# First feed-forward: a fourth pair of blocks by seven products, five low parts a group summed by DMA from DRAM

## The chip, the cores and the metric

The kernel runs on one core of a Trainium2 chip. The metric is the device time of one execution in microseconds (us), the median of several. Products run on TensorE (PE; PEld is its loading of weights), sums and splits on VectorE (DVE), casts and scalings on ScalarE (ACT). GpSimd (POOL) issues the DMAs that sum while they write, and SyncE (SP) issues the loads.

## What is computed

One layer of a streaming encoder on 256 tokens of width 2048, in float32:

```python
def swiglu_ffn(h, w_in, w_out):
    gate, up = jnp.split(h @ w_in, 2, axis=-1)
    return (jax.nn.silu(gate) * up) @ w_out

x = x + 0.5 * swiglu_ffn(rms_norm(x, ffn1_norm), ffn1_w_in, ffn1_w_out)   # F = 5632
...                                  # convolution and gating mixers, then cross-attention
x = x + 0.5 * swiglu_ffn(rms_norm(x, ffn2_norm), ffn2_w_in, ffn2_w_out)
return rms_norm(x, final_norm)
```

The change is in `h @ w_in` of the first feed-forward, a product of 256 x 2048 by 2048 x 11264.

## The kernel before

**Split numbers.** A float32 weight tile `raw` (128 x 1024) is split into a high part, which ScalarE casts (L339), and a low part, which VectorE gets as raw - high (L340); both go into a buffer of two planes, `hl`. A product is three matmuls: high x by high w, high x by low w, low x by high w (`three`, `by_two`). x is split once, in `x_hl`.

**Groups.** The 11264 columns are taken in 11 groups of 512 gate and 512 up columns. A group runs over 16 k-tiles of 128 rows, which are eight pairs. Group 0 is plain. In groups 1 to 10 each pair has a letter in `PATTERNS`. A "C" pair (`eight`) takes eight products of 128 tokens by 512 columns, 24 matmuls. An "S" pair (`seven`) takes seven products of sums of blocks, 21 matmuls: VectorE forms sums of weight blocks first (L385, L386, L391, L398) and then splits those too, in three and a half splits. The matching sums of x blocks (`forms`) are made once during group 0, by `sides`.

**Summed low parts.** For the k-tiles in `SUMMED`, which lie in C pairs, VectorE does nothing: ScalarE writes -raw into the low plane (L355) and the cast into the high plane (L356), and a DMA issued by GpSimd adds raw to the low plane, from raw's own buffer (L357). There is one such buffer, `hl_s`; the next k-tile of the list is begun when the matmuls of the one before have been written out.

**Buffers.** Raw tiles come into four buffers of `wraw` and five pieces of `spare`, nine in turn. Splits go to three buffers of `whl` and two of `ring`, five in turn. All eight banks of PSUM hold accumulators, named by the products: "5", "6", "7" and "1" are complete after the last S pair, "2", "3", "4" and "8" after the last pair. VectorE drains the latter four (L449, four instructions a group) and `give` makes the group's output `h`. x itself, `xT` (2 MB), stays in SBUF from group 0 to the output product, which adds to it.

**Order.** The program is written in this order, and a scheduler then fixes the order of each engine's queue when the kernel is built; each queue runs in that order. A waiting instruction holds up what stands behind it on its engine.

Of the kernel before, what the change touches and what calls it, by code (L numbers as in the profile page):

```python
# [17 lines left out]
P = 128  # L18
D = 2048
T = 256  # L20
# [15 lines left out]

PATTERNS = ("SCSCSCCC", "SCSCSCCC")

SUMMED = (2, 7, 13)

# [26 lines left out]
def layer(ctx: ExitStack, tc: tile.TileContext, a: dict):  # L67
# [231 lines left out]
    class FeedForward:  # L299
# [5 lines left out]

        def __init__(self, stack, tags, x_hl, gain, w_in, pattern):
            self.x_hl, self.gain, self.w_in, self.pattern = x_hl, gain, w_in, pattern
            self.tags = tags
            self.spairs = [p for p, c in enumerate(pattern) if c == "S"]
# [20 lines left out]
            self.hA = self.hB = self.hC = None  # L330
            self.hl = self.own.tile([P, 2, 1024], F32R, name="hl_s")
            self.first = self.hl.rearrange("p a (f two n) -> p (a f) two n", f=2, two=2)

        def parts(self, raw, n=1024, last=False):

            i = self.at % 5
            self.at += 1
            hl = whl.tile([P, 2, 1024], F32R, name="hl") if last or i < 3 else self.ring[i - 3]
            nc.scalar.copy(out=hl[:, 0, :n], in_=raw[:, :n])  # L339
            newest[0] = nc.vector.tensor_tensor(  # L340
                out=hl[:, 1, :n], in0=raw[:, :n], in1=hl[:, 0, :n].bitcast(F32), op=ALU.subtract
            )
            return hl
# [7 lines left out]

        def summed(self, j, k):

            raw = self.raw(j, k)
            nc.scalar.activation(out=self.hl[:, 1], in_=raw, func=AF.Copy, scale=-1.0)  # L355
            nc.scalar.copy(out=self.hl[:, 0], in_=raw)  # L356
            nc.gpsimd.dma_start(out=self.hl[:, 1], in_=raw, accum_op=ALU.add)  # L357

# [43 lines left out]
        def eight(self, j, p, b, first, last, plain):  # L402
            for k in (2 * p, 2 * p + 1):
                at = (j, k) in self.sums_at and self.sums_at.index((j, k))
                w = self.parts(self.raw(j, k), last=plain) if at is False else self.hl
# [15 lines left out]
        def group(self, j, r, after=()):  # L421
# [10 lines left out]
            for p, c in enumerate(self.pattern):  # L432
# [8 lines left out]
                else:  # L441
                    late = p > self.spairs[-1] and len(after) > 0
                    self.eight(j, p, b, p == self.pattern.index("C"), p == n - 1, late)
                    if p > self.spairs[-1] + 1:
                        for _ in range(2):
# [5 lines left out]

        def run(self, before, after, root):
            acc = token_accs()
            self.sums_at = [(j, k) for j in range(1, NG) for k in SUMMED if j < NG - 1 or k < SUMMED[-1]]
            for k in range(KD):
# [64 lines left out]
    with ExitStack() as stack:  # L520
        ff = FeedForward(stack, ("S1", "S0", "S2"), x_hl, "ffn1_norm", a["ffn1_w_in"], PATTERNS[0])

# [19 lines left out]

        turns = ff.run(x_arrives, x_more, x_root)

# [419 lines left out]
    with ExitStack() as stack:  # L964
        ff = FeedForward(stack, ("S0", "S1", "S2"), x_hl, "ffn2_norm", a["ffn2_w_in"], PATTERNS[1])
        x2 = ff.x2
# [162 lines left out]
```

## Time and profile before

| | us |
|---|---|
| median of 3 runs (2112.79 to 2116.53) | 2114.3 |
| the profiled execution | 2113.83 |
| its span | 2111.8 |
| TensorE busy in the span | 2084.6 |
| VectorE busy | 1576.2 |
| ScalarE busy | 1156.1 |
| groups 1 to 10 of the first feed-forward | about 55 to 478 |
| groups 1 to 10 of the second feed-forward | about 1434 to 1853 |

Times in the profile count from the start of the span. A row of a timeline has the start, the length, the engine, the line, the operation, what it writes and reads, and in brackets how long the engine was idle before it and which instruction ended that. A row of waits has the engine and line that waited, what it waited for, and us in total, times, and the longest.

### The profile page before, as it was taken

The page shows a single profiled execution, that of the slowest core. Times are in us where ns is not written, and L with a number is a line of the kernel's source. Part 1 is how long each engine was busy: PE and PEld are TensorE (multiplying, and loading weights), DVE is VectorE, ACT ScalarE, POOL GpSimd, SP SyncE. Part 2 cuts the span into 40 slices and gives each one's busy share as a digit, 9 for nine tenths or more (in the row PEclk, how much of TensorE's full clock was granted, in tenths as well). Part 3 has the DMA queues.
Part 4 walks back from the last instruction along what each step waited for, and adds up shares of the span by engine and source line. Part 5 has one row for each costly group of instructions (what it writes and reads, how often), then busy time and mean ns, then how long its engine had stood idle before and what let it go on. Part 6 is the DMA issues. An engine that isn't in the chain of part 4 may idle for free.

```text
span 2111.8 us, 26657 instructions
## 1 busy us (share of the span) xinstructions
PE 2084.6 (99%) x9764; PEld 1737.2 (82%) x9764; DVE 1576.2 (75%) x2215; ACT 1156.1 (55%) x1450; POOL 66.4 (3%) x81
## 2 busy tenths in 40 slices
PE   8999999999999999999999999999999999999998
PEld 6888877888888888888888888888888888888886
DVE  7887888876655589989877665777878888787754
ACT  7656565655544455444764454556665666454443
POOL 0000000000000000000000000000000000000000
PEclk9999999999999999999999999999999999999999
DMA  9788777855666676656565543686788778656664
GB/s 352 219 239 231 238 239 216 262 171 168 218 191 189 201 238 204 187 177 186 174 201 187 184 156 111 206 281 190 232 253 249 217 230 263 180 160 201 195 192 149
DMA packets 121955, 440.24 MB, mean 208 GB/s; under 512 B 13664, under 2 KB 13792, under 8 KB 121696
## 3 DMA queue, kind: packets, MB, share of 16 engines
q1 hardware_dynamic: 113184, 407.35, 59.9%
q0 software_dynamic: 8352, 30.41, 7.8%
q8 instruction: 76, 1.25, 0.2%
q10 hardware_dynamic: 288, 0.79, 0.1%
q14 instruction: 55, 0.45, 0.1%
HBM read 405.99 MB, written 2.10 MB: 193 GB/s over the span
## 4 chain that ended last, share of the span: by engine, by line
PE 70%; issue 25%; DMA 2%; DVE 2%; POOL 1%; ACT 1%; POOLq 0%; SPq 0%; DVEq 0%; ACTq 0%
PE acc L172 12%; PE acc L173 12%; PE acc L171 12%; PE acc L125 8%; PE acc L126 4%; PE acc L288 4%; PE acc L289 4%; PE acc L291 4%; PE aux L263 1%; PE acc L275 1%; PE acc L277 1%; PE acc L276 1%; DMA raw<-in_ffn_w_in 1%; POOL hl_s L357 1%; PE acc L1049 1%
## 5 line engine op out<-in xcount | busy, mean ns | idle before, releaser
L113 DVE TENSOR_TENSOR hl<-raw,hl 128x1024 fp32r<-128x1024 f32 (+1 forms) x402 | 489.0, 1217 | 280.9 <-ACT hl L112 279.8
L112 ACT CAST hl<-raw 128x1024 fp32r<-128x1024 f32 (+1 forms) x402 | 419.6, 1045 | 482.6 <-PE acc L173 300.1
L339 ACT CAST hl<-spare 128x1024 fp32r<-128x1024 f32 (+1 forms) x148 | 143.7, 996 | 117.0 <-DVE spare L386 55.0
L340 DVE TENSOR_TENSOR hl<-spare,hl 128x1024 fp32r<-128x1024 f32 (+1 forms) x148 | 169.7, 1158 | 32.8 <-ACT hl L339 32.2
L288 PE MATMUL acc<-hl,x_hl 128*128 128x512 f32 x440 | 152.7, 392 | 8.3 <-ACT hl L339 8.3
L289 PE MATMUL acc<-hl,x_hl 128*128 128x512 f32 x440 | 159.0, 392 | 0.1
L339 ACT CAST ring<-spare 128x1024 fp32r<-128x1024 f32 (+1 forms) x106 | 103.3, 983 | 97.7 <-DVE spare L386 49.8
L340 DVE TENSOR_TENSOR hl<-raw,hl 128x1024 fp32r<-128x1024 f32 (+1 forms) x106 | 119.6, 1133 | 47.7 <-ACT hl L339 47.0
L339 ACT CAST hl<-raw 128x1024 fp32r<-128x1024 f32 (+1 forms) x106 | 101.9, 975 | 65.4 <-DVE raw L398 27.6
L291 PE MATMUL acc<-hl,x_hl 128*128 128x512 f32 x440 | 136.7, 391 | 0.0
L340 DVE TENSOR_TENSOR ring<-spare,ring 128x1024 fp32r<-128x1024 f32 (+1 forms) x106 | 120.4, 1142 | 21.3 <-ACT ring L339 20.8
L288 PEld LDWEIGHTS acc<-hl,x_hl 128*128 128x128 f32 x440 | 83.0, 189 | 25.8 <-ACT hl L339 8.7
L172 PE MATMUL acc<-hl,x_hl 128*128 128x512 f32 x256 | 100.5, 392 | 0.5 <-DVE hl L113 0.5
L172 PE MATMUL acc<-hl,m_hl 128*128 128x512 f32 x256 | 100.3, 392 | 0.0
L173 PE MATMUL acc<-hl,m_hl 128*128 128x512 f32 x256 | 100.2, 391 | 0.0
L173 PE MATMUL acc<-hl,x_hl 128*128 128x512 f32 x256 | 99.8, 390 | 0.0
L289 PEld LDWEIGHTS acc<-hl,x_hl 128*128 128x128 f32 x440 | 82.9, 189 | 17.9 <-DVE hl L340 0.8
L291 PEld LDWEIGHTS acc<-hl,x_hl 128*128 128x128 f32 x440 | 83.2, 189 | 17.5
L289 PE MATMUL acc<-ring,x_hl 128*128 128x512 f32 x256 | 92.6, 389 | 0.5 <-DVE ring L340 0.5
L171 PE MATMUL acc<-hl,m_hl 128*128 128x512 f32 x256 | 91.2, 392 | 0.0
L125 PE MATMUL acc<-x_hl,hl 128*128 128x512 f32 x256 | 91.0, 398 | 0.0
L125 PE MATMUL acc<-y_hl,hl 128*128 128x512 f32 x256 | 90.5, 399 | 0.0
(326 smaller groups left out, 5066.5 us busy)
## 6 DMA issues: line engine op xcount, KB each, us to landing
spare<-in_ffn_w_in SPq DMA_DIRECT2D x192, 512.0 KB, 5.2
raw<-in_ffn_w_out SPq DMA_DIRECT2D x176, 512.0 KB, 3.8
raw<-in_ffn_w_in SPq DMA_DIRECT2D x160, 512.0 KB, 4.9
hl_s<-spare POOLq DMA_DIRECT2D x32, 512.0 KB, 4.9
raw<-in_w_mix_vg SPq DMA_DIRECT2D x32, 512.0 KB, 4.7
raw<-in_w_k SPq DMA_DIRECT2D x32, 512.0 KB, 3.9
raw<-in_w_v SPq DMA_DIRECT2D x32, 512.0 KB, 4.3
raw<-in_w_mix_out SPq DMA_DIRECT2D x32, 512.0 KB, 4.6
```

Source lines behind the costliest of these rows:

```text
L112: nc.scalar.copy(out=hl[:, 0, :size], in_=raw[:, :size])
L113: newest[0] = nc.vector.tensor_tensor(out=hl[:, 1, :size], in0=raw[:, :size], in1=hl[:, 0, :size].bitcast(F32), op=ALU.subtract)
L125: nc.tensor.matmul(acc, lhsT=w_hi, rhs=x_hl, start=first, stop=False, skip_group_check=True)
L126: nc.tensor.matmul(acc[:, 0], lhsT=w_lo, rhs=x_hl[:, 0], start=False, stop=last, skip_group_check=True)
L171: nc.tensor.matmul(acc[t], lhsT=x[:, 0, s], rhs=hi[:, k], start=k0 + k == 0, stop=False)
L172: nc.tensor.matmul(acc[t], lhsT=x[:, 0, s], rhs=lo[:, k], start=False, stop=False)
L173: nc.tensor.matmul(acc[t], lhsT=x[:, 1, s], rhs=hi[:, k], start=False, stop=k0 + k == nk - 1)
L288: nc.tensor.matmul(acc[t][g], lhsT=x[:, 0, s], rhs=hi[:, cols[g]], start=(t, g) in first, stop=False)
L289: nc.tensor.matmul(acc[t][g], lhsT=x[:, 0, s], rhs=lo[:, cols[g]], start=False, stop=False)
L291: nc.tensor.matmul(acc[t][g], lhsT=x[:, 1, s], rhs=hi[:, cols[g]], start=False, stop=last)
L339: nc.scalar.copy(out=hl[:, 0, :n], in_=raw[:, :n])
L340: newest[0] = nc.vector.tensor_tensor(out=hl[:, 1, :n], in0=raw[:, :n], in1=hl[:, 0, :n].bitcast(F32), op=ALU.subtract)
```

## The change

Pair 5 of the first feed-forward becomes an S pair, so four of eight are. Five k-tiles a group, 2, 6, 12, 14 and 15, have their low part summed by DMA, where three had (2, 7, 13). The summing DMA reads the weights again from DRAM, in both feed-forwards. After group 0, x's place is given to a sixth split buffer and a second summed buffer (tile `more`), and x is loaded again after the last group. The second feed-forward keeps its pattern, its list and its single buffers. Line numbers after L339 move up by 3 or more: the drains are L452, the summing DMA is L360.

```diff
-PATTERNS = ("SCSCSCCC", "SCSCSCCC")
+PATTERNS = ("SCSCSSCC", "SCSCSCCC")
-SUMMED = (2, 7, 13)
+SUMMED = ((2, 6, 12, 14, 15), (2, 7, 13))
...
-            self.hl = self.own.tile([P, 2, 1024], F32R, name="hl_s")
+            self.hls = [self.own.tile([P, 2, 1024], F32R, name="hl_s")]
...
         def parts(self, raw, n=1024, last=False):
-            i = self.at % 5
+            i = self.at % (3 + len(self.ring))
...
-        def summed(self, j, k):
-            raw = self.raw(j, k)
-            nc.scalar.activation(out=self.hl[:, 1], in_=raw, func=AF.Copy, scale=-1.0)
-            nc.scalar.copy(out=self.hl[:, 0], in_=raw)
-            nc.gpsimd.dma_start(out=self.hl[:, 1], in_=raw, accum_op=ALU.add)
+        def summed(self, at):
+            if at >= len(self.sums_at):
+                return
+            j, k = self.sums_at[at]
+            raw, hl = self.raw(j, k), self.hls[at % len(self.hls)]
+            nc.scalar.activation(out=hl[:, 1], in_=raw, func=AF.Copy, scale=-1.0)
+            nc.scalar.copy(out=hl[:, 0], in_=raw)
+            nc.gpsimd.dma_start(out=hl[:, 1], in_=self.w_in[j, :, k], accum_op=ALU.add)
...
-                if at is not False and at + 1 < len(self.sums_at):
-                    self.summed(*self.sums_at[at + 1])
+                if at is not False:
+                    self.summed(at + len(self.hls))
...
-                    self.summed(*self.sums_at[0])
+                    self.summed(0)
+            if more is not None:
+                more()
+                self.summed(1)
...
-            if k in (6, 9, 12):
+            if k in (6, 9, 12, 15):
                 ff.sides(k // 3 - 2)
...
-        turns = ff.run(x_arrives, x_more, x_root)
+        def x_given():
+            more = xt.tile([P, 4, 1024], F32R, name="more", tag="x")
+            ff.ring.append(more[:, :2])
+            ff.hls.append(more[:, 2:])
+
+        turns = ff.run(x_arrives, x_more, x_root, x_given)
+        xT = xt.tile([P, KD, T], F32, name="xT", tag="x")
+        for k in range(0, KD, 8):
+            nc.gpsimd.dma_start(out=xT[:, k:k + 8], in_=a["xT"][:, k:k + 8])
```

How the order of the queues changes is shown at three places. The first is TensorE where group 1 of the first feed-forward ends and group 2 begins (L275 to L277 are S matmuls, L288 to L291 C matmuls; `aux` and `acc` are accumulators; `DMASW` stands for a summing DMA). Before, behind the last C matmuls of group 1, stand the S matmuls of group 2's first pair into banks that are free early (the first four rows are their end), and then, from the fifth row on, the first ones into a drained bank:

```order
L277 MATMUL aux<-hl,ring 128x512
L275 MATMUL acc<-hl,x_hl 128x512
L276 MATMUL acc<-hl,x_hl 128x512
L277 MATMUL acc<-hl,x_hl 128x512
L275 MATMUL acc<-hl,x_hl 128x512 [waits DVE_49,Activation_49]
L276 MATMUL acc<-hl,x_hl 128x512
L277 MATMUL acc<-hl,x_hl 128x512
L288 MATMUL acc<-hl_s,x_hl 128x512 [waits Activation_49]
L289 MATMUL acc<-hl_s,x_hl 128x512 [waits DMASW3_49]
```

Now group 1's last k-tile, summed, stands behind group 2's first twelve matmuls, and the first matmul into a drained bank follows at once:

```order
L275 MATMUL acc<-hl,x_hl 128x512 [waits DVE_49]
L276 MATMUL acc<-hl,x_hl 128x512
L277 MATMUL acc<-hl,x_hl 128x512
L288 MATMUL acc<-hl_s,x_hl 128x512 [waits Activation_49]
L288 MATMUL acc<-hl_s,x_hl 128x512 x3
L289 MATMUL acc<-hl_s,x_hl 128x512 [waits DMASW4_49]
L289 MATMUL acc<-hl_s,x_hl 128x512
L291 MATMUL acc<-hl_s,x_hl 128x512 x2
L289 MATMUL acc<-hl_s,x_hl 128x512 x2
L291 MATMUL acc<-hl_s,x_hl 128x512 x2
L275 MATMUL acc<-hl,x_hl 128x512 [waits DVE_49]
```

The matmuls into banks that are free early moved ahead of the last k-tile, so fewer of them stand between the end of a bank and its next use. The second place is GpSimd, the first five summing DMAs. Before, each reads the buffer of the raw tile and waits for ScalarE and for the load:

```order
L357 DMA hl_s<-spare 128x1024 [waits DMAHW0_49,Activation_49]
L357 DMA hl_s<-raw 128x1024 [waits DMAHW3_49,Activation_49]
L357 DMA hl_s<-spare 128x1024 [waits DMAHW2_49,Activation_49]
L357 DMA hl_s<-raw 128x1024 [waits DMAHW5_49,Activation_49]
L357 DMA hl_s<-spare 128x1024 [waits DMAHW0_49,DVE_49,Activation_49]
```

Now they read DRAM, into two buffers in turn, and wait for ScalarE alone, but for the first into x's place:

```order
L360 DMA hl_s<-in_ffn_w_in 128x1024 [waits Activation_49]
L360 DMA more<-in_ffn_w_in 128x1024 [waits DMAHW3_49,DMAHW2_49,DMAHW4_49,DMAHW0_49,DMAHW7_49,DVE_49,Activation_49]
L360 DMA hl_s<-in_ffn_w_in 128x1024 [waits Activation_49]
L360 DMA more<-in_ffn_w_in 128x1024 [waits Activation_49]
L360 DMA hl_s<-in_ffn_w_in 128x1024 [waits Activation_49]
```

The raw tile's buffer is no longer tied to the DMA. The third place is TensorE inside an S pair. Before, in the second pair of its kind in group 2, the three matmuls of a product stand together (L275, L276, L277):

```order
L275 MATMUL acc<-hl,ring 128x512 [waits Activation_49]
L276 MATMUL acc<-hl,ring 128x512 [waits DVE_49]
L277 MATMUL acc<-hl,ring 128x512
L275 MATMUL aux<-hl,ring 128x512
L276 MATMUL aux<-hl,ring 128x512
L277 MATMUL aux<-hl,ring 128x512
L275 MATMUL aux<-hl,ring 128x512 [waits Activation_49]
L276 MATMUL aux<-hl,ring 128x512 [waits DVE_49]
L277 MATMUL aux<-hl,ring 128x512
L275 MATMUL acc<-hl,x_hl 128x512
L276 MATMUL acc<-hl,x_hl 128x512
L277 MATMUL acc<-hl,x_hl 128x512
```

Now, in pair 5 of group 6, right behind the S pair 4, the matmuls that need only the high part (L275) stand alone ahead of those that need VectorE's low part:

```order
L275 MATMUL acc<-more,ring 128x512 [waits Activation_49]
L275 MATMUL aux<-more,ring 128x512
L288 MATMUL acc<-more,x_hl 128x512
L275 MATMUL aux<-hl,ring 128x512 [waits Activation_49]
L276 MATMUL acc<-more,ring 128x512 [waits DVE_49]
L277 MATMUL acc<-more,ring 128x512
L276 MATMUL aux<-more,ring 128x512
L277 MATMUL aux<-more,ring 128x512
L275 MATMUL acc<-hl,x_hl 128x512
L276 MATMUL aux<-hl,ring 128x512 [waits DVE_49]
L277 MATMUL aux<-hl,ring 128x512
L276 MATMUL acc<-hl,x_hl 128x512
```

The matmuls on low parts moved behind others that could be issued without them.

More of the change, by code (lines that the diff above doesn't have):

```diff
@@ L299, in layer, with __init__ @@
     class FeedForward:
-        def __init__(self, stack, tags, x_hl, gain, w_in, pattern):
+        def __init__(self, stack, tags, x_hl, gain, w_in, pattern, summed):
             self.x_hl, self.gain, self.w_in, self.pattern = x_hl, gain, w_in, pattern
-            self.tags = tags
+            self.tags, self.pattern_sums = tags, summed
             self.spairs = [p for p, c in enumerate(pattern) if c == "S"]
@@ L330, in __init__ @@
             self.hA = self.hB = self.hC = None
-            self.hl = self.own.tile([P, 2, 1024], F32R, name="hl_s")
-            self.first = self.hl.rearrange("p a (f two n) -> p (a f) two n", f=2, two=2)
+            self.hls = [self.own.tile([P, 2, 1024], F32R, name="hl_s")]
+            self.first = self.hls[0].rearrange("p a (f two n) -> p (a f) two n", f=2, two=2)
         def parts(self, raw, n=1024, last=False):
-            i = self.at % 5
+            i = self.at % (3 + len(self.ring))
             self.at += 1
@@ L404, in eight @@
                 at = (j, k) in self.sums_at and self.sums_at.index((j, k))
-                w = self.parts(self.raw(j, k), last=plain) if at is False else self.hl
+                w = self.parts(self.raw(j, k), last=plain) if at is False else self.hls[at % len(self.hls)]
                 begin = [(1, 1)] if first and k % 2 == 0 else []
@@ L450, in group, with run @@
             self.give(j, (p1, u2), (u4, u5), r)
-        def run(self, before, after, root):
+        def run(self, before, after, root, more=None):
             acc = token_accs()
-            self.sums_at = [(j, k) for j in range(1, NG) for k in SUMMED if j < NG - 1 or k < SUMMED[-1]]
+            sums = self.pattern_sums
+            self.sums_at = [(j, k) for j in range(1, NG) for k in sums if j < NG - 1 or k < min(14, sums[-1])]
             for k in range(KD):
@@ L964, in layer @@
     with ExitStack() as stack:
[L965 removed]
+        ff = FeedForward(stack, ("S0", "S1", "S2"), x_hl, "ffn2_norm", a["ffn2_w_in"], PATTERNS[1], SUMMED[1])
         x2 = ff.x2
```

4 lines of the change are left out of this document (2 added, 2 removed).

## The prediction

> **What bounds the kernel now.** I read the page first, then the time by stretches, the waits of TensorE, and last the order of time around the two places that the change touches. From the page:
>
> ```profile
> span 2111.8 us, 26657 instructions
> PE 2084.6 (99%) x9764; PEld 1737.2 (82%) x9764; DVE 1576.2 (75%) x2215; ACT 1156.1 (55%) x1450; POOL 66.4 (3%) x81
> ```
>
> TensorE is busy nearly throughout, so a matmul that goes is worth its whole pace, as long as its suppliers keep up. Stretches: a saturated piece of group 0, then groups 1 to 10 of the first and of the second feed-forward (columns: length; busy time of PE, PEld, DVE, ACT, POOL; granted clock, which is full; DMA share; GB/s).
>
> ```profile
> 15.00:30.00 15.00, 15.00 (x68) 12.42 (x67) 14.05 (x28) 14.63 (x26) 0.00 (x0) 1.00 1.03 403
> 55.20:478.20 423.00, 417.76 (x1842) 344.42 (x1842) 339.06 (x405) 249.56 (x279) 24.27 (x28) 1.00 0.76 227
> 1434.00:1857.00 423.00, 420.84 (x1862) 347.68 (x1861) 341.49 (x410) 252.73 (x283) 24.29 (x28) 1.00 0.76 228
> ```
>
> In the first feed-forward TensorE idles 423.0 - 417.8 = 5.2 us, in the second 2.2. The waits of TensorE there (us in total, times, longest), of the first and then of the second feed-forward:
>
> ```profile
> PE acc L275 <- DVE spare L449: 4.7, 4, 2.7
> PE acc L289 <- DVE ring L340: 0.5, 1, 0.5
> ```
>
> ```profile
> PE acc L275 <- DVE spare L449: 2.2, 3, 1.3
> ```
>
> So all but 0.5 us is the group boundary: the next group's first matmul into an accumulator waits for VectorE's drain of that accumulator. Nothing waits for a summing DMA.
>
> **The matmuls that go.** One of five ordinary pairs becomes a seven-product pair: 21 matmuls instead of 24, in ten groups, 30 fewer. The first matmuls of groups 1 and 2:
>
> ```profile
> 55.24 0.39 PE L275 MATMUL acc<-hl,ring 128*128 128x512 f32 x1
> 96.72 0.39 PE L275 MATMUL acc<-hl,ring 128*128 128x512 f32 x1
> ```
>
> 183 matmuls in 41.48 us are 0.2267 us each (the 0.39 is pipeline depth). 30 x 0.2267 = **-6.8 us**. A group falls to 180 x 0.2267 = 40.8 us.
>
> **VectorE and ScalarE.** The spacing of their instructions is read from start to start, VectorE's first, then ScalarE's:
>
> ```profile
> 349.01 0.68 DVE L385 TENSOR_TENSOR spare<-spare 128x512 f32<-128x512 f32 x1
> 349.61 0.69 DVE L386 TENSOR_TENSOR spare<-spare 128x512 f32<-128x512 f32 x1
> 350.21 1.22 DVE L340 TENSOR_TENSOR hl<-spare,hl 128x1024 fp32r<-128x1024 f32 x1
> 351.35 0.68 DVE L391 TENSOR_TENSOR spare<-spare 128x512 f32<-128x512 f32 x1
> ```
>
> ```profile
> 201.56 1.06 ACT L355 ACTIVATE hl_s<-raw 128x1024 fp32r<-128x1024 f32 x1
> 202.52 1.03 ACT L356 CAST hl_s<-raw 128x1024 fp32r<-128x1024 f32 x1
> ```
>
> VectorE: 0.60 for 512 columns, 1.14 for 1024. A seven-product pair costs it four sums, three whole splits and a half one, 5 x 0.60 + 3 x 1.14 = 6.4 us, where an ordinary pair cost two splits, 2.3. Two more summed tiles take 2.3 off. Net +1.9 a group: from 33.9 (339.06 / 10) to 35.8 of 40.8, 88%. ScalarE: 0.96 an instruction; four casts (one of them half) instead of two, +1.5, and one more instruction for each added sum, +1.9: from 25.0 to 28.4 of 40.8. Both still fit, so they cost nothing by sum; what covers them is VectorE's idle time, which falls from 8.4 to 5.0 us a group (the third rival).
>
> **The drains at the boundary.** In the order of the changed kernel, the number of matmuls between the last one into the first accumulator and the next group's first into it is 6, 10, 8, 14, 14, 14, 16, 6 and 17 at the nine boundaries; it was 20 at all. Less 0.39 for the last matmul and 0.7 for the drain, the cushion was 3.4 us and becomes 0.2 to 2.7. How late VectorE comes today, at the first boundary and at the worst, the seventh, with the wait that followed there:
>
> ```profile
> 96.27 0.61 PE L291 MATMUL acc<-ring,x_hl 128*128 128x512 f32 x2
> 97.34 2.47 DVE L449 TENSOR_TENSOR spare<-spare,acc 128x512 f32<-128x512 f32 x4
> ```
>
> ```profile
> 348.75 0.62 PE L291 MATMUL acc<-ring,x_hl 128*128 128x512 f32 x2
> 354.00 2.47 DVE L449 TENSOR_TENSOR spare<-spare,acc 128x512 f32<-128x512 f32 x4
> 354.83 0.47 PE L275 MATMUL acc<-hl,x_hl 128*128 128x512 f32 x1 [2.74 <-DVE spare L449]
> ```
>
> The first accumulator's last matmul is six before the pair shown, 1.36 us, and ends 0.47 after its start, so the drain could have begun 0.9 before the L291 row: it came 2.0 and 6.1 us late. Over the nine boundaries the lateness read this way is 0.1 to 6.1, mean 3.0. With this lateness set against the new cushions (mean over all pairings) the stalls would be 15.9 us, +11.2. But k-tiles 14 and 15 are now summed, which takes two splits, 2.3 us, out of VectorE's queue just ahead of the drains: with lateness 2.3 less the stalls are 4.1, -0.6; none at all is the lower end, -4.7. I take **+1.5**, near the second, since those splits do stand there, but above it, since VectorE has less idle time to catch up.
>
> One cause of late work is seen 60 us before the worst boundary, in the chain that ended last (start, length):
>
> ```profile
> 287.18 8.59 DMA hl_s<-spare
> 295.77 0.02 issue
> 295.79 3.80 DMA spare<-in_ffn_w_in
> ```
>
> A load waited for a buffer that a summing DMA was still reading. The load queue lost time this way 24 times in the groups of the first feed-forward:
>
> ```profile
> SPq L349 <- DMA hl_s<-spare: 31.8, 11, 5.7
> SPq L349 <- DMA hl_s<-raw: 29.9, 13, 6.8
> ```
>
> The change removes this edge, since the DMA now reads DRAM and the buffer is free after ScalarE's copy. It does so in the second feed-forward too, whose order of matmuls is otherwise unchanged: of its 2.2 us between all and nothing go, I take half, **-1.1**.
>
> **The summing chain.** When the last matmul on a low part is done, ScalarE writes the negative (row 201.56 above), POOL issues, the sum lands:
>
> ```profile
> 203.01 0.88 POOL L357 DMA_DIRECT2D hl_s<-raw  x1 [12.78 <-ACT hl_s L355]
> DMA to landing us min/median/max: 4.5/4.8/9.9
> ```
>
> 0.44 + 1.45 + 4.8 = 6.7 us, or 30 matmuls. In the new order 27 to 102 matmuls lie between the last use of a buffer and the first use of the sum that follows in it (k-tile 15 is close behind 12 in the same buffer); only the 27 is short, by **+0.6**. In the second feed-forward the least is 43. Here the source moves from SBUF to DRAM, which no row shows. From both sides: no change, or the landing of loads in a saturated stretch, 8.4 us (below), which makes 16 leads too short, by 24.8 us in all. I take 4.8, since over the whole page plain loads from DRAM land no later than sums from SBUF (KB each, median us to landing):
>
> ```profile
> raw<-in_ffn_w_in SPq DMA_DIRECT2D x160, 512.0 KB, 4.9
> hl_s<-spare POOLq DMA_DIRECT2D x32, 512.0 KB, 4.9
> ```
>
> The Trainium skill speaks against it: "DMA: Bandwidth & Descriptors", section "Latency and other measured facts", puts HBM access at 0.2 us on average but 2 us at high load and calls HBM the slowest target. By an estimate from that page the landing would be 6.8 and the shortfalls 7.0 us, so the sum below would end at 2115.2. No run here shows a sum from DRAM.
>
> **Traffic.** A stretch in which the DMA engines are full and one sum is under way, 36.75 to 40.75 us (packets, MB, share), and then the issues of loads in 10 to 45 us with their landing:
>
> ```profile
> q0 software_dynamic: 141, 0.52, 65.6%
> q1 hardware_dynamic: 165, 0.60, 39.7%
> ```
>
> ```profile
> raw<-in_ffn_w_in SPq DMA_DIRECT2D x7, 512.0 KB, 8.4
> ```
>
> At 403 GB/s the 0.60 MB of loads take 1.5 of the 4.0 us, so a sum costs 2.5, a load of 0.52 MB 1.3. A group needs 16 x 1.3 + 4.8 x 2.5 = 32.8 of 40.8 us (27.8 of 41.5 before). If a sum cost another load's 1.3, 39.0: still under. Hidden, with the nine load buffers as cover. x comes back in two transfers of 1 MB behind the last group and is first needed some 75 us later: nothing.
>
> **Entry.** Group 0 gains a load, a sum and the fourth set of x combinations while the queues are full; between nothing and 1.3 + 2.5 us reach TensorE, which waited 1.2 there today. I take **+0.8**.
>
> ```profile
> 43.86 1.19 PE L288 MATMUL acc<-hl,x_hl 128*128 128x512 f32 x4 [1.22 <-ACT hl L339]
> ```
>
> **Sum.** -6.8 + 1.5 - 1.1 + 0.6 + 0.8 = -5.0 on the profiled execution's 2113.8 (span 2111.8 and 2.0 around it; the median of the runs, 2114.3, is 0.5 above): **2108.8 us**.
>
> **Rivals.** *All waits go* (13%): with free load buffers, a sixth split buffer and a second summed one, VectorE is never late; -6.8 - 5.2 - 2.2 gives 2099.6, or about 2101 with the entry. For it: the edge above. Against it: the cushions.
>
> *Sums land late* (19%): halfway between 4.8 and the 8.4 of saturated loads, 6.6, six leads (27 to 37 matmuls) are too short, by 5.8 us in all instead of 0.6: 2114.0; at 8.4, 24.8 instead of 0.6: 2133. For it: DRAM is read by loads at the same time. Against it: the two medians of 4.9.
>
> *VectorE becomes the bound* (18%; the other side). Its waits in groups 1 to 10 today, over 34 us on loads and 45 on ScalarE:
>
> ```profile
> DVE hl L340 <- ACT hl L339: 32.8, 37, 2.9
> DVE spare L385 <- DMA spare<-in_ffn_w_in: 16.6, 5, 4.7
> DVE ring L340 <- ACT ring L339: 12.1, 16, 2.9
> DVE spare L385 <- DMA raw<-in_ffn_w_in: 9.5, 4, 5.8
> DVE spare L386 <- DMA raw<-in_ffn_w_in: 7.3, 3, 4.1
> ```
>
> That is 7.9 us a group, on top of 35.8 of work: 43.7. The place is pairs 4 and 5, two seven-product pairs in a row: 42 matmuls, 9.5 us, for which VectorE needs 12.8. It decides when the waits do not shrink below 6.2, for today's group is 42.0; at 6.9 the ten groups take 427 instead of 420: 2121. For it: in the new order TensorE takes first parts alone, as one does who has caught up, in 11 to 27 places a group instead of 2 to 4. Against it: waits shrink when there is more to do, and the seven-product pair is preceded by pair 3, which leaves VectorE 4.3 us spare.
>
> **Chances.** Forecast 50% (2104 to 2112). Of it 0.44 lies below 2110.1, the bound of 0.2% that a measurement of this kernel can tell. Faster 0.44 + 0.13 = 0.57; within 0.2% 0.06 + 0.14 (late sums) + 0.03 = 0.23; slower 0.15 + 0.05 = 0.20. The range 2100 to 2122 leaves out the worst of the last two rivals and the best of the first.
>
> **What would show it.** Matmuls down by 30 and ten groups in about 413 to 417 us; the wait of TensorE on the drain (now L452) at 4 to 9 us in total; no wait of the load queue on summing DMAs; landing of sums from DRAM about 5 us; VectorE near 36 us a group. The prediction is wrong if sums land at 7 us or more, or if first matmuls inside pairs 4 and 5 wait for the splits of L340.

## The result, and the profile after

The changed kernel takes **2142.9 us** (median of 6 runs, 2137.9 to 2149.1), the kernel before on the same chip 2115.3 (6 runs, 2112.8 to 2118.0): ratio **1.0136**, 95% interval 1.0120 to 1.0151. The forecast was 2108.8 with a range of 2100 to 2122. The profiled execution took 2140.1 us. Its page, two lines:

```profile
span 2138.3 us, 26636 instructions
PE 2090.8 (98%) x9734; PEld 1738.1 (81%) x9734; DVE 1596.2 (75%) x2261; ACT 1196.1 (56%) x1492; POOL 84.3 (4%) x102
```

Thirty matmuls fewer, as foreseen, in a span that is 26.5 us longer. All of it lies in groups 1 to 10 of the first feed-forward. The row of that stretch (length; busy time of PE, PEld, DVE, ACT, POOL; clock; DMA share; GB/s):

```profile
55.00:504.20 449.20, 422.26 (x1808) 344.03 (x1807) 359.23 (x449) 282.18 (x317) 41.19 (x48) 0.97 0.83 239
```

449 us instead of 423, TensorE idle for 27.0 of them instead of 5.2, and the granted clock 0.97 instead of 1.00. In the second feed-forward TensorE did not wait at all (2.2 before). What TensorE waited for in the stretch (us in total, times, longest):

```profile
PE acc L289 <- DMA more<-in_ffn_w_in: 12.5, 4, 4.3
PE acc L289 <- DMA hl_s<-in_ffn_w_in: 7.5, 3, 4.1
PE acc L275 <- ACT hl L339: 4.0, 1, 4.0
PE acc L275 <- DVE spare L452: 2.3, 1, 2.3
```

Waits on sums, 20.0 us, where there were none; the drains (L452) cost 2.3 instead of 4.7. The page's DMA issues (KB each, median us to landing) show the sums, and the loads beside them, which took 5.2 and 4.9 before:

```profile
spare<-in_ffn_w_in SPq DMA_DIRECT2D x192, 512.0 KB, 6.6
raw<-in_ffn_w_in SPq DMA_DIRECT2D x160, 512.0 KB, 6.0
hl_s<-in_ffn_w_in POOLq DMA_DIRECT2D x53, 512.0 KB, 7.6
```

In this stretch the sums of both buffers landed after 7.8 us (median), against 4.8 before.

**A second loss behind the waits.** The timeline of TensorE at the first long wait (start, length, count, idle before):

```profile
101.65 1.22 PE L289 MATMUL acc<-hl_s,x_hl 128*128 128x512 f32 x2 [4.06 <-DMA hl_s<-in_ffn_w_in]
102.67 1.05 PE L291 MATMUL acc<-hl_s,x_hl 128*128 128x512 f32 x2
...
105.23 0.63 PE L275 MATMUL acc<-hl,x_hl 128*128 128x512 f32 x1
105.66 0.63 PE L276 MATMUL acc<-hl,x_hl 128*128 128x512 f32 x1
...
107.21 0.39 PE L276 MATMUL acc<-hl,ring 128*128 128x512 f32 x1
107.44 0.39 PE L277 MATMUL acc<-hl,ring 128*128 128x512 f32 x1
```

From 101.65 to about 107 us a matmul starts every 0.43 us, then every 0.23. The same place in stretches of 5 us (behind the five engines stand the granted clock, the DMA share and GB/s):

```profile
95.00:100.00 5.00, 2.60 (x12) 1.82 (x10) 0.75 (x2) 1.66 (x2) 0.86 (x1) 1.00 0.94 233
100.00:105.00 5.00, 3.35 (x8) 2.67 (x9) 1.66 (x3) 1.43 (x2) 0.00 (x0) 0.52 1.04 282
105.00:110.00 5.00, 5.00 (x20) 3.99 (x19) 5.00 (x8) 4.74 (x6) 0.87 (x1) 0.80 0.93 257
```

The clock fell to half for one such stretch. In five of eleven windows of 41.5 us it was 0.92 or 0.96 instead of 1.00; the missing shares (0.08 + 0.08 + 0.04 + 0.04 + 0.04) of 41.5 us are 11.6 us. The starts of the matmuls say the same: what the slow ones among them took beyond 0.2267 us each comes to 11.7. It also fits the stretch: 1800 matmuls x 0.2267 = 408.1, with 27.0 of waits 435.1, and the stretch took 449.2, 14.1 more; the same count leaves 2.9 over in the kernel before (1830 x 0.2267 + 5.2 = 420.1 of 423.0).

### The profile page after: what moved, and what is told of

Its sections match the earlier page's. It is cut to its first block, busy times and chain, and to the rows that moved or that the text cites. A ratio compares the mean times of both kernels' runs of the same rounds, so it can differ in the third digit from the quotient of the medians.

```text
span 2138.3 us, 26636 instructions
## 1 busy us (share of the span) xinstructions
PE 2090.8 (98%) x9734; PEld 1738.1 (81%) x9734; DVE 1596.2 (75%) x2261; ACT 1196.1 (56%) x1492; POOL 84.3 (4%) x102
## 4 chain that ended last, share of the span: by engine, by line
PE 83%; issue 11%; DMA 3%; ACT 1%; POOL 1%; DVE 1%; SPq 0%; POOLq 0%; DVEq 0%; ACTq 0%
PE acc L172 12%; PE acc L173 12%; PE acc L171 12%; PE acc L125 8%; PE acc L289 7%; PE acc L291 6%; PE acc L288 6%; PE acc L126 4%; PE acc L276 2%; PE acc L277 2%; PE acc L275 2%; PE aux L263 1%; PE aux L276 1%; PE aux L277 1%; PE aux L275 1%
## 5 line engine op out<-in xcount | busy, mean ns | idle before, releaser
L113 DVE TENSOR_TENSOR hl<-raw,hl 128x1024 fp32r<-128x1024 f32 (+1 forms) x402 | 488.6, 1216 | 284.2 <-ACT hl L112 283.0
L112 ACT CAST hl<-raw 128x1024 fp32r<-128x1024 f32 (+1 forms) x402 | 419.6, 1045 | 485.5 <-PE acc L173 300.4
L339 ACT CAST hl<-spare 128x1024 fp32r<-128x1024 f32 (+1 forms) x138 | 133.8, 990 | 92.9 <-DVE spare L389 49.8
L340 DVE TENSOR_TENSOR hl<-spare,hl 128x1024 fp32r<-128x1024 f32 (+1 forms) x138 | 157.2, 1147 | 32.4 <-ACT hl L339 31.4
L339 ACT CAST ring<-spare 128x1024 fp32r<-128x1024 f32 (+1 forms) x99 | 96.7, 981 | 75.0 <-DVE spare L389 23.9
L340 DVE TENSOR_TENSOR hl<-raw,hl 128x1024 fp32r<-128x1024 f32 (+1 forms) x96 | 106.0, 1109 | 33.7 <-ACT hl L339 33.1
L340 DVE TENSOR_TENSOR ring<-spare,ring 128x1024 fp32r<-128x1024 f32 (+1 forms) x99 | 111.7, 1133 | 16.4 <-ACT ring L339 15.9
L339 ACT CAST hl<-raw 128x1024 fp32r<-128x1024 f32 (+1 forms) x96 | 91.2, 960 | 56.4 <-DVE raw L401 15.1
L288 PE MATMUL acc<-hl,x_hl 128*128 128x512 f32 x324 | 113.8, 394 | 8.5 <-ACT hl L339 8.5
L289 PE MATMUL acc<-hl,x_hl 128*128 128x512 f32 x324 | 117.5, 393 | 0.1
L172 PE MATMUL acc<-hl,x_hl 128*128 128x512 f32 x256 | 100.5, 392 | 0.5 <-DVE hl L113 0.5
L291 PE MATMUL acc<-hl,x_hl 128*128 128x512 f32 x324 | 100.4, 391 | 0.0
L173 PE MATMUL acc<-hl,x_hl 128*128 128x512 f32 x256 | 99.8, 390 | 0.0
L360 POOL DMA_DIRECT2D hl_s<-in_ffn_w_in x53 | 46.3, 873 | 1207.1 <-DMA spare<-in_ffn_w_in 623.7
L125 PE MATMUL acc<-o_hl,hl 128*128 128x512 f32 x256 | 90.4, 399 | 0.0
L171 PE MATMUL acc<-hl,x_hl 128*128 128x512 f32 x256 | 90.1, 392 | 0.2 <-ACT hl L112 0.2
L289 PE MATMUL acc<-hl_s,x_hl 128*128 128x512 f32 x212 | 81.3, 398 | 7.5 <-DMA hl_s<-in_ffn_w_in 7.5
```

What stands on the lines that cost most here:

```text
L112: nc.scalar.copy(out=hl[:, 0, :size], in_=raw[:, :size])
L113: newest[0] = nc.vector.tensor_tensor(out=hl[:, 1, :size], in0=raw[:, :size], in1=hl[:, 0, :size].bitcast(F32), op=ALU.subtract)
L125: nc.tensor.matmul(acc, lhsT=w_hi, rhs=x_hl, start=first, stop=False, skip_group_check=True)
L171: nc.tensor.matmul(acc[t], lhsT=x[:, 0, s], rhs=hi[:, k], start=k0 + k == 0, stop=False)
L172: nc.tensor.matmul(acc[t], lhsT=x[:, 0, s], rhs=lo[:, k], start=False, stop=False)
L173: nc.tensor.matmul(acc[t], lhsT=x[:, 1, s], rhs=hi[:, k], start=False, stop=k0 + k == nk - 1)
```

## The experiments

Each is one or two edits of the kernel before or of the changed kernel; "against before" is the ratio to the kernel before on the same chip. A lead is the number of matmuls between the last use of a summed buffer and the first use of the next sum in it. "Shortfall" is worked out from each kernel's order on TensorE: leads below 43 matmuls (0.44 + 1.45 + 7.8 = 9.7 us), each by what it lacks, in us. It takes 7.8 us of landing for every kernel, though the sums of some landed later, after up to 9.0 us (median, e9_place). "VectorE on loads" and "TensorE" are the sums of their rows of waits from 97 to 470 us, from group 2 on; in the slower kernels group 10 ends after that. The runs were spread over several chips, on which the kernel before took 2112.2 to 2116.4 us, so two kernels are compared by their ratios where the chips differ.

| kernel | seven-product pairs; sums; load buffers | shortfall | VectorE on loads | TensorE | us | against before |
|---|---|---|---|---|---|---|
| before | 3; 3 from SBUF; 9 | 0 | 32.2 | 5.2 | 2115.3 | 1 |
| e3_source | 3; 3; 9 | 0 | 19.3 | 0.4 | 2107.0 | 0.9948 (0.9931 to 0.9965) |
| e9_place | 3; 3; 9 | 0 | 17.7 | 0 | 2108.2 | 0.9977 (0.9967 to 0.9986) |
| **after** | 4; 5; 9 | 16.1 | 40.7 | 26.5 | 2142.9 | 1.0136 (1.0120 to 1.0151) |
| e1b_list | 4; 5, other list; 9 | 2.7 | 54.5 | 30.2 | 2151.7 | 1.0152 (1.0123 to 1.0180) |
| e2_sbuf | 4; 5 from SBUF; 9 | - | 70.4 | 37.5 | 2167.1 | 1.0225 (1.0194 to 1.0256) |
| e4_three | 4; 3; 9 | 0 | 35.8 | 25.0 | 2141.2 | 1.0106 (1.0078 to 1.0135) |
| e10_five | 3; 5; 9 | 8.0 | 76.7 | 27.5 | 2149.5 | 1.0179 (1.0158 to 1.0200) |
| e7_spread | 4 apart; 3; 9 | 0 | 35.0 | 14.1 | 2125.6 | 1.0061 (1.0044 to 1.0078) |
| e11_spread4 | 4 apart; 4; 9 | 0 | 49.1 | 22.5 | 2140.0 | 1.0130 (1.0113 to 1.0146) |
| e8_loads | 4; 3; 11 | 0 | 5.6 | 5.6 | 2120.1 | 1.0033 (1.0019 to 1.0047) |
| e12_list11 | 4; 5, other list; 11 | 4.6 | 20.2 | 7.9 | 2122.3 | 1.0047 (1.0032 to 1.0061) |
| e17_own11 | 4; 5, own list; 11 | 27.1 | 22.2 | 31.2 | 2158.8 | 1.0205 (1.0190 to 1.0220) |
| e13_mix | 4 apart; 3; 11 | 0 | 7.1 | 3.5 | 2117.2 | 1.0020 (1.0011 to 1.0030) |
| e15_entry | 4 apart; 3; 11, later | 0 | 12.4 | 5.2 | 2112.0 | 0.9989 (0.9979 to 0.9999) |
| e16_seven | 3; 3; 7 | 4.0 | 58.9 | 20.7 | 2175.9 | 1.0296 (1.0275 to 1.0317) |

### First theory: sums land late into short leads (A)

**e1b_list**, longer leads with as many sums:

```diff
-SUMMED = ((2, 6, 12, 14, 15), (2, 7, 13))
+SUMMED = ((2, 3, 7, 13, 15), (2, 7, 13))
```

> The changed kernel with another list of five summed k-tiles, 2, 3, 7, 13 and 15: the same number of sums from DRAM, of splits, of matmuls. Only the leads differ: between the last use of a summed buffer and the first use of its next sum there are at least 38 matmuls, where the changed kernel has 27 and ten leads below 41. Theory A (sums from DRAM land after 7.4 to 7.8 us, so 0.44 + 1.45 + 7.8 = 9.7 us or 43 matmuls are needed, and each wait near 4 us is followed by some 4 us of matmuls at half pace): sum waits of TensorE fall from 20.0 to at most 4 us, no matmuls at half pace, 2108 to 2118 us. Rival B (VectorE is the bound, 35.9 us of work a group) and rival C (the traffic of five more reads a group slows everything): nothing that they count changes, 2135 us or more.

2151.7 us, and 25.9 us of waits on sums in 13 places (groups 1 to 10), where the leads leave 2.7 at a landing of 7.8, and at most some 10, by an estimate from the leads in its trace, at 8.3 (its own sums landed after 7.9 and 8.3). Theory A alone has fallen.

**e2_sbuf**, the source back in SBUF:

```diff
-            nc.gpsimd.dma_start(out=hl[:, 1], in_=self.w_in[j, :, k], accum_op=ALU.add)
+            nc.gpsimd.dma_start(out=hl[:, 1], in_=raw, accum_op=ALU.add)
```

> The changed kernel with the summing DMA reading the raw tile's own buffer again, in both feed-forwards. In its order the least lead is 31 matmuls, 7.0 us. Theory A: landing back at 4.8 us, 6.7 us needed, so no wait on a sum over 1 us and no half pace; but the load queue waits for the summing DMAs again, now five a group (60 us or more in all), so VectorE may come later to the drains: 2108 to 2122 us. Rival B (VectorE is the bound): 2135 us or more, with later loads more than now. Rival C (traffic from DRAM): about 2115 too, but then the landing of a sum in the second feed-forward stays where it was in the changed kernel.

2167.1 us: reading DRAM was the better half of the change. In groups 1 to 10 the sums from SBUF landed after a median of 6.7 us into `hl_s` and 8.2 into `more`, though 4.8 in the second feed-forward, so the late landing is not the source's alone; and the load queue waited 176 us (97 to 470) for DMAs, where it waits 2.5 in the changed kernel.

**e3_source**, the kernel before with the DRAM source alone:

```diff
-            nc.gpsimd.dma_start(out=self.hl[:, 1], in_=raw, accum_op=ALU.add)
+            nc.gpsimd.dma_start(out=self.hl[:, 1], in_=self.w_in[j, :, k], accum_op=ALU.add)
```

> The kernel before with one part of the change alone: the summing DMA reads DRAM, in both feed-forwards. The least lead is 43 matmuls, 9.75 us. Theory A: sums land after about 7.5 us, which the leads just cover, so no wait on sums over 1 us; the load queue no longer waits for summing DMAs, so the drains come no later than before: 2110 to 2116 us, beside 2115. Rival C (reads from DRAM by the sums cost time by themselves): 2120 us or more.

**2107.0 us, faster than both kernels**, and the best that these runs found. All that TensorE waited for in groups 1 to 10:

```profile
PE acc L289 <- DMA hl_s<-in_ffn_w_in: 0.4, 1, 0.4
```

The drains' 4.7 us are gone, although sums land after 7.2 and loads after 6.3 us here (4.9 and 5.2 before).

**e4_three**, the fourth pair with three sums:

```diff
-SUMMED = ((2, 6, 12, 14, 15), (2, 7, 13))
+SUMMED = ((2, 7, 13), (2, 7, 13))
```

> The changed kernel with three summed k-tiles a group, 2, 7 and 13, in two buffers in turn: four seven-product pairs stay. The leads in the first feed-forward become 59 to 108 matmuls; VectorE has two more splits a group, 35.9 + 2.3 = 38.2 of 40.8 us. Theory A: no wait on sums and no half pace, but the drains come later, by up to 2.3 us at each boundary: 2108 to 2120 us. Rival B (VectorE is the bound: 38.2 of work and several us of waits a group): 2150 us or more.

2141.2: no wait on a sum in these groups, leads of 59 and more, and as slow as the changed kernel. TensorE now waits for splits and casts; the waits of VectorE in the ten groups (us in total, times, longest) begin with ScalarE and four on loads:

```profile
DVE hl L340 <- ACT hl L339: 18.3, 21, 2.8
DVE spare L388 <- DMA spare<-in_ffn_w_in: 16.2, 7, 4.7
DVE spare L388 <- DMA raw<-in_ffn_w_in: 8.2, 2, 4.8
DVE spare L389 <- DMA spare<-in_ffn_w_in: 7.7, 3, 3.1
DVE spare L389 <- DMA raw<-in_ffn_w_in: 6.2, 4, 4.0
```

### Second round: two pairs in a row (D), load buffers (E), the number of sums (F)

**e10_five**, the changed kernel without the fourth pair:

```diff
-PATTERNS = ("SCSCSSCC", "SCSCSCCC")
+PATTERNS = ("SCSCSCCC", "SCSCSCCC")
...
-            if k in (6, 9, 12, 15):
+            if k in (6, 9, 12):
```

> The changed kernel with three seven-product pairs again (pattern SCSCSCCC): five sums from DRAM a group, the second summed buffer, the sixth split buffer and x's reload stay. The least lead is 31 matmuls, five leads below 41. VectorE has 33.9 - 2.3 = 31.6 us of work a group. Theory D (two seven-product pairs in a row, 4 and 5, ask VectorE for 12.8 us plus 2.5 of drains where TensorE needs 9.5, and what is then late runs on into the sums): no loss of this kind, 2106 to 2114 us. Theory E (nine load buffers are too few when four pairs hold two raw tiles each): the same. Theory F (five sums from DRAM cost by their landing, their traffic or ScalarE): 2130 us or more.

2149.5 us: five sums do the harm without a fourth pair, and VectorE, with only 31.6 us of work a group, waits longest of all for loads. How such a wait becomes one on a sum is seen ahead of the longest. VectorE's timeline:

```profile
209.29 1.22 DVE L340 TENSOR_TENSOR ring<-spare,ring 128x1024 fp32r<-128x1024 f32 x1
220.14 0.69 DVE L388 TENSOR_TENSOR spare<-raw 128x512 f32<-128x512 f32 x1 [9.62 <-DMA raw<-in_ffn_w_in]
```

The loads issued into `raw` from 205 to 222 us (KB each, median us to landing):

```profile
raw<-in_ffn_w_in SPq DMA_DIRECT2D x3, 512.0 KB, 12.7
```

ScalarE's timeline behind that:

```profile
222.60 1.05 ACT L339 CAST hl<-spare 128x1024 fp32r<-128x1024 f32 x1 [4.47 <-DVE spare L389]
...
230.74 0.62 ACT L339 CAST ring<-raw 128x512 fp32r<-128x512 f32 x1 [3.41 <-DVE raw L401]
231.27 1.06 ACT L358 ACTIVATE more<-spare 128x1024 fp32r<-128x1024 f32 x1
```

The sum's DMA in the chain (start, length), and then TensorE's timeline:

```profile
232.73 9.83 DMA more<-in_ffn_w_in
```

```profile
242.61 1.22 PE L289 MATMUL acc<-more,x_hl 128*128 128x512 f32 x2 [5.98 <-DMA more<-in_ffn_w_in]
```

VectorE stands 9.6 us for a raw tile. ScalarE, whose queue is in order, stands behind VectorE twice (4.5 and 3.4 us), and the sum's first instruction (L358) stands behind those casts. So the sum is begun late and lands late, and TensorE's wait bears the sum's name. The load was late by its landing: it was issued at 207.4 us and landed 12.7 later, as one of six loads and two sums issued from 204 to 211 us, and the DMA engines were full behind them (columns as in the stretches above):

```profile
210.00:220.00 10.00, 9.53 (x43) 7.54 (x41) 0.52 (x1) 3.39 (x4) 0.89 (x1) 1.00 1.02 288
```

Just ahead of that, up to 200.4 us, the load queue had stood 5.2 us for a buffer (`SPq L349 <- DVE spare L401`). That the stop made the burst is likely, but not shown. In the changed kernel the waits read alike: ahead of the one at 242.18 VectorE waited 3.2 us for a load, ScalarE 4.0 for VectorE, and L358 ran behind it.

**e7_spread**, four pairs, none beside another (and the last group's helper called four times behind its last pair):

```diff
-PATTERNS = ("SCSCSSCC", "SCSCSCCC")
+PATTERNS = ("SCSCSCSC", "SCSCSCCC")
-SUMMED = ((2, 6, 12, 14, 15), (2, 7, 13))
+SUMMED = ((2, 7, 11), (2, 7, 13))
```

> Four seven-product pairs, but none beside another within a group (pattern SCSCSCSC), with three summed k-tiles (2, 7, 11) in two buffers, so that leads are 78 matmuls or more; compare with the kernel of three sums and the pattern SCSCSSCC, 2141.2 us. VectorE's work is the same, 38.2 of 40.8 us a group. Theory D (the two pairs in a row): most of the loss goes, 2105 to 2122 us. Theory E (load buffers) and B (VectorE's total): 2130 us or more.

2125.6, 15.6 less than e4_three with the same work (0.45%, or 9.5 us, by the ratios): between the two expectations. Where the pairs stand matters, but VectorE waits for loads as before, 35.0 us.

**e11_spread4**, the same with `SUMMED[0] = (3, 7, 11, 15)`:

> As the spread pattern SCSCSCSC, with four summed k-tiles a group (3, 7, 11, 15), one in each ordinary pair: least lead 43 matmuls, VectorE 37.0 of 40.8 us. Theory D: 2100 to 2115 us, the fastest of the kernels with four such pairs. Theory E: 2130 us or more. Theory F (sums cost): slower than the three-sum kernel with the same pattern.

2140.0: one more sum costs 14 us, though only 0.2 us of waits on sums are left (least lead 43) and VectorE has less to do. Its waits for loads rise from 35.0 to 49.1.

**e8_loads**, e4_three with two more load buffers in place of the sixth split buffer:

```diff
...
-            more = xt.tile([P, 4, 1024], F32R, name="more", tag="x")
-            ff.ring.append(more[:, :2])
-            ff.hls.append(more[:, 2:])
+            loads = xt.tile([P, 2, 1024], F32, name="loads", tag="x0")
+            ff.raws.extend(loads[:, i] for i in range(2))
+            ff.hls.append(xt.tile([P, 2, 1024], F32R, name="more", tag="x1"))
...
```

> The kernel of four seven-product pairs and three sums (2141.2 us) with the sixth split buffer turned into two more load buffers, eleven in all; sums, leads (95 or more) and pattern as there. x is kept in two halves of its place for that. Theory E (load buffers): VectorE's waits for loads, 38 us in groups 2 to 10, fall to under 15, and the time to 2105 to 2125 us. Theory D (two pairs in a row) and B (VectorE's total): 2132 us or more, or slower by the split buffer that is missing.

2120.1, 21 less (0.73%, or 15 us, by the ratios). All of VectorE's waits for loads from 97 to 500 us, to be set against the four such rows of e4_three above:

```profile
DVE spare L388 <- DMA spare<-in_ffn_w_in: 2.7, 2, 1.4
DVE spare L388 <- DMA raw<-in_ffn_w_in: 2.0, 1, 2.0
...
DVE spare L389 <- DMA raw<-in_ffn_w_in: 0.9, 1, 0.9
```

38 us (35.8 from 97 to 470) have become 5.6, with the pairs in a row as before. Theory E holds for the larger part. The edit also takes the sixth split buffer away, and the scheduler's order changes with it; no run adds load buffers alone.

### Third round: the load buffers from several sides

**e12_list11**, e1b_list with the edit of e8_loads:

> The kernel of four seven-product pairs (SCSCSSCC) and five sums of the list 2, 3, 7, 13, 15 (2151.7 us) with the sixth split buffer turned into two more load buffers, eleven in all; leads 34 or more, seven of them below 43. Theory E (load buffers: a summed k-tile holds its load buffer until TensorE is done with the earlier sum, the load queue stops behind it, and VectorE then waits for loads): 2115 to 2130 us, VectorE's waits for loads (60 us in groups 2 to 10 without the two buffers) under 20. Theory F (the number of sums costs by itself, through traffic, landing or ScalarE): 2140 us or more.

2122.3 instead of 2151.7 (1% or 22 us by the ratios), by two load buffers: with long leads and enough load buffers five sums cost little more than three (2120.1). VectorE's waits for loads are 20.2 us, a little above what was expected. The waits on sums (97 to 470 us) are nearly gone:

```profile
PE acc L289 <- DMA more<-in_ffn_w_in: 5.3, 5, 1.7
PE acc L289 <- DMA hl_s<-in_ffn_w_in: 0.8, 3, 0.3
```

Traffic and late landing alone are not the cause, then: the DMA engines were busier here than in the changed kernel (0.88 against 0.86 of that time), and the sums landed later (medians 8.1 and 8.5 us, against 7.8).

**e9_place**, the changed kernel with `PATTERNS[0] = "SCSCSCCC"` and `SUMMED[0] = (2, 7, 13)` (and without the fourth set of x combinations, as e10_five):

> The changed kernel with the old pattern (SCSCSCCC) and the old list (2, 7, 13): what stays is the DRAM source, the second summed buffer and the sixth split buffer in x's place, and x's reload. Theory E: three sums hold load buffers no more than in the kernel before with the DRAM source (2107 us): 2105 to 2113 us. Theory G (what stands in x's place costs by itself, at the entry above all): 2118 us or more.

2108.2: no wait of TensorE from 97 to 470 us, although the sums landed later than in the changed kernel (medians 9.0 and 8.6 us, against 7.8): the leads are long, 105 matmuls and more for `hl_s` in the trace. What stands in x's place costs little: 1 us beside e3_source, 6 us (0.29%) by the ratios, whose intervals lie just apart.

**e13_mix**, e7_spread with the edit of e8_loads, and the second buffer's first sum later:

```diff
                     self.seven(j, p, b, p == 0, p == self.spairs[-1])
+                    if j == 1 and p == 0 and len(self.hls) > 1:
+                        self.summed(1)
...
                 more()
-                self.summed(1)
```

> The spread pattern SCSCSCSC with three sums (2, 7, 11; 2125.6 us), eleven load buffers instead of the sixth split buffer, and the first sum into the second summed buffer begun only behind group 1's first pair, so that its load does not hold up the others while x is still in use. Theories D (two pairs in a row) and E (load buffers) together, each for a part of the loss: 2097 to 2108 us, TensorE's waits in groups 1 to 10 under 5 us. If only one of them holds, no better than 2112 us.

2117.2, 9 above the range, and among the times expected if only one theory holds. But groups 2 to 10 are nearly free of waits (3.5 us), with about 38 us of VectorE's work a group, and beside e8_loads (2120.1) it no longer matters much that the pairs stand apart. What is lost lies at the entry, seen in two stretches of 41.5 us (columns as above):

```profile
15.00:56.50 41.50, 39.08 (x164) 31.07 (x163) 24.03 (x42) 29.01 (x44) 1.88 (x2) 0.96 1.03 384
56.50:98.00 41.50, 38.43 (x158) 30.96 (x157) 33.52 (x41) 26.99 (x30) 2.61 (x3) 0.92 0.61 188
```

**e15_entry**, the same with x's place given away behind group 1's first pair:

```diff
-                    if j == 1 and p == 0 and len(self.hls) > 1:
+                    if j == 1 and p == 0 and self.more is not None:
+                        self.more()
                         self.summed(1)
...
-            if more is not None:
-                more()
+            self.more = more
```

> The kernel of the spread pattern, three sums and eleven load buffers (2117.2 us) with x's place given away only behind group 1's first pair, not at the end of group 0. In that kernel TensorE lost about 10 us at the entry: it waited 2.4 us at 42.7 and 3.1 at 61.5, each followed by matmuls at half pace, and did 322 matmuls from 15 to 98 us where 366 fit; a load issued at 27.8 took 13.8 us. Theory E2 (the two added buffers let the load queue run further ahead while the DMA engines are full, and what is needed first lands late): most of the 10 us comes back, 2106 to 2111 us. If the entry is lost by the order of VectorE's queue (group 0's output ahead of the first sums): no change, 2115 us or more.

2112.0, half of the 10 us and 1 us above the first range's end; the entry, in the same two windows:

```profile
15.00:56.50 41.50, 39.27 (x168) 30.95 (x167) 29.77 (x50) 30.85 (x46) 1.01 (x1) 1.00 0.95 364
56.50:98.00 41.50, 41.50 (x184) 34.37 (x183) 34.54 (x43) 27.79 (x32) 3.49 (x4) 1.00 0.86 247
```

352 matmuls instead of 322, at full clock. This is the best kernel found with a fourth pair, and it is 0.1% faster than before (the interval ends just short of no change); e3_source, with three, is 0.5% faster.

### Last round: both causes apart

**e17_own11**, the changed kernel with its own list and the edit of e8_loads:

> The changed kernel with its own list (2, 6, 12, 14, 15) and eleven load buffers instead of nine and a sixth split buffer. Its order has short leads still, 20 to 42 matmuls in 14 places, where 43 cover a landing of 7.8 us. Theory E (load buffers): VectorE's waits for loads in groups 2 to 10 fall from 41 us to 20 or less, and with them most of the loss: 2118 to 2128 us. Theory A (short leads times late landing): the waits on sums stay at 20 us or more, as 27 us of shortfall are worked out from the order: 2135 us or more. In between, each has its part.

2158.8. VectorE's waits for loads fell as theory E says, from 40.7 to 22.2 us, and the waits on sums stayed, as theory A says (97 to 470 us):

```profile
PE acc L289 <- DMA hl_s<-in_ffn_w_in: 17.6, 7, 4.8
PE acc L289 <- DMA more<-in_ffn_w_in: 10.2, 5, 4.4
```

27.8 us, against 27.1 worked out from leads and a landing of 7.8. VectorE was less late: it stood 19.6 us for TensorE (`DVE spare L452 <- PE acc L291`). Here mainly the leads are left, and their arithmetic gives the size; that it agrees to 0.7 us is partly luck, since this kernel's own sums landed after 8.2 and 8.3 us.

**e16_seven**, e3_source with two load buffers fewer:

```diff
-            self.raws = [spare[:, i * 1024:(i + 1) * 1024] for i in (5, 0, 1, 2, 3)]
+            self.raws = [spare[:, i * 1024:(i + 1) * 1024] for i in (5, 0, 1)]
```

> The kernel before with the DRAM source (2107.0 us) and seven load buffers instead of nine, in both feed-forwards; pattern, list and summed buffer as before. Theory E: VectorE's waits for loads in groups 2 to 10 rise from 19 us to 40 or more, TensorE waits, and each feed-forward loses some 15 to 40 us: 2135 to 2190 us. If load buffers do not bind: 2107 to 2115 us.

2175.9, 69 us more in two feed-forwards (73 by the ratios), by an edit of nothing but two load buffers; the leads in the new order are little shorter (shortfall 4.0).

## Why the prediction was wrong, step by step

**The matmuls that go: right.** 9734 instead of 9764 in the records, -6.8 us.

**VectorE and ScalarE: right in work, 35.9 and 28.2 us a group (35.8 and 28.4 foreseen).** VectorE's work is not the bound of the changed kernel: it stood 24.4 us for TensorE ahead of the drains, and e13_mix has about 38 us of its work a group with 3.5 us of TensorE's waits. The third rival, VectorE's work with its waits on top, did not decide here. Its sign shows in e4_three, where TensorE waits for splits and casts: from 97 to 470 us VectorE worked 312.9 us and waited 35.8 for loads and 20.1 for ScalarE, 368.8 of the 373. With 5.6 us of waits for loads (e8_loads) the same work leaves 5.6 us of TensorE's waits instead of 25.0. That much the same waits for loads (32.2 us) did little harm before, beside 300.1 us of work, fits this, but no run holds the two apart.

**The drains: wrong in direction.** I let these waits grow from 5.2 to 6.7 us, by shorter cushions; they fell to 2.3. In e3_source, with the cushions as before, they are gone (0.4 us is left, on a sum), so the lateness that I carried over seems to have come from the edge that the change removes. **The second feed-forward: right**, -2.2 for -1.1. **The entry: right**, 0.5 us (a wait of TensorE at 56.48 for ScalarE's output, L418) for 0.8.

**The load queue no longer waits for summing DMAs: right** (67.4 us before, 2.5 now for all DMAs, 97 to 470 us).

**The summing chain: one of the two steps that failed.** I took 4.8 us of landing and so +0.6. It was 7.8, which the leads in the new order fall short of by 16.1 us, and the waits on sums were 20.0. The argument for 4.8, that plain loads from DRAM landed no later than sums from SBUF, was an argument from another kind of transfer: in e3_source, where nothing else changed, the sum's landing rose from 4.9 to 7.2 and the loads' with it, from 5.2 to 6.3. The rival "sums land late" named the mechanism; its table (5.8 us at 6.6, 24.8 at 8.4) holds 7.8's 16.1 between its rows, though even its worst time, 2133, lies below the 2140.1 measured, for it has no term for the clock. The Trainium skill's "DMA: Bandwidth & Descriptors", section "Latency and other measured facts", from which I had estimated 6.8, pointed the right way; the medians measured, 7.2 in e3_source, 7.8 in the changed kernel and up to 9.0 in e9_place, lie above.

**Traffic, "Hidden, with the nine load buffers as cover": the other step that failed.** I counted the bytes and not how long a load buffer is held. The bytes came out low too: 27.8 of 41.5 us for the kernel before is 0.67, where the row shown with it has a DMA share of 0.76, and the changed kernel's share of 0.83 is 37.3 us a group, not 32.8. But more of it did no harm in e12_list11. With nine buffers VectorE waited 41 us for loads in the changed kernel and 35 to 77 in its neighbours, and whatever then stood next in an in-order queue was late: splits in e4_three, sums in e10_five and e1b_list. With eleven, e4_three and e1b_list lose 15 and 22 us less (by the ratios); with seven even the untouched pattern loses 69 more. Why a fourth pair and the fourth and fifth sums hold buffers longer was not isolated: the load queue waits for one buffer or another in every kernel for most of the time (315 us of 373 in e9_place, 319 in e10_five), so its rows don't tell. e10_five with eleven buffers was not run.

**A term that was missing: the clock.** 11.6 us beside the waits: I priced a wait at its length alone.

**The two causes do not add.** Longer leads alone (e1b_list) or more load buffers alone (e17_own11) left the kernel as slow (1.0152 for 1.0136, with intervals that overlap) or made it slower (1.0205, 15 us), for the other cause was still there (in e17_own11 with more shortfall, 27.1 for 16.1, and a wait of 3.7 us at the entry); both together (e12_list11, 1.0047) took 19 off. In the changed kernel itself the share of each in its 20.0 us can't be told from these runs.

**The sum again, with what was measured:** 2108.8 - 0.6 + 20.0 for the sums, + 11.6 for the clock, + 4.0 for a late cast, - 4.4 for the drains, - 1.1 for the second feed-forward, - 0.3 for the entry: 2138.0, where the profiled execution took 2140.1.

**What would have been the better change** was inside it: I gave the DRAM source -1.1 us, since I counted it only where nothing else changed. Alone it is worth 0.5%, 11 us by the ratio (5.2 us between the two profiled spans).

## What to carry to other kernels

Count buffers by time, not by number: at 16 loads in 40.8 us, nine buffers come round every 23 us, and landing, waiting and use must fit into that; when a change makes tiles stay longer or land later, look first at what the engine that consumes loads waits for. A wait on TensorE named after a DMA may be a late load two in-order queues away: follow it back until an engine was idle for something that no engine made. And when a change has several parts, cost each part alone: here the one that was a side effect was the only gain.

## What the hardware showed beyond that

After waits of about 4 us TensorE ran at half pace for some 5 us (4.06 us up to 101.65, clock 0.52 in the window from 100 to 105; 4.3 to 5.3 us behind each of the four longest waits, which lost 1.8 to 2.6 us by it), so such a wait cost half as much again; waits of 2.18 and 2.87 us at 330 and 375 us were followed by no slow matmul, but one of 2.18 at 417.72 was, with the clock at 0.76 from 415 to 420. The Trainium skill, "TensorE: Matmul & The Clock Gate", "Part 1: The HAM clock gate", puts the fall to half rate behind an idle window of 3.4 us and says that the window runs free of the kernel; the long waits agree, and the short one at 417.72 goes beyond it.

Sums from SBUF land late as well where there are many: 6.7 and 8.2 us into the two buffers in e2_sbuf, 4.8 in its second feed-forward with one buffer and three sums. Why was not tried.
